# All modulation products on TensorE in float32, spread over four column bands

## The chip, the core and the metric

The kernel runs on one core of a Trainium2 chip. The core has five engines with a queue each: TensorE (PE in the profile; its weight loads are PEld), VectorE (DVE), ScalarE (ACT), GpSimd (POOL) and SyncE (SP), whose queue issues the transfers. The metric is the device time of one execution in microseconds; the figure of a kernel is the median of its runs.

## The reference, cut to what matters

Two layers work on 256 latent tokens and 256 context tokens of width 1024. In each layer a conditioning vector for the latents (`c`) and one for the context (`c_ctx`) give six modulation vectors of 1024 numbers: shift, scale and gate of the token mixing (parts 0, 1, 2) and of the channel mixing (parts 3, 4, 5).

```
silu_c, silu_cc = silu(c), silu(c_ctx)
for l in range(2):
    sh1, sc1, g1, sh2, sc2, g2 = split(silu_c @ w_mod[l] + b_mod[l], 6)      # latents
    csh1, csc1, cg1, ... = split(silu_cc @ w_mod[l] + b_mod[l], 6)           # context
    h = layer_norm(x) * (1 + sc1) + sh1
    x = layer_norm(ALPHA * x + g1 * token_mixer(h @ w_in[l]))
    h = layer_norm(x) * (1 + sc2) + sh2
    x = layer_norm(ALPHA * x + g2 * channel_mixer(h))
```

`w_mod[l]` is 1024 x 6144 in float32. The token mixer joins a Hyena, a Conformer and an S5 branch; the channel mixer is a dense SwiGLU in layer 0 and eight SwiGLU experts, two per token, in layer 1. In layer 1 only the latents are carried on behind the token mixer.

## The kernel before

All large products are three float32r products each: operands are split into a high part (a copy on ACT, line 123) and a low part (a subtraction on DVE, line 124), and lines 131 to 133 issue high-high, low-high and high-low. `p` tiles are the input projection, `bo` the branch outputs, `fo` and `pa` the two sides of the feed-forward.

A modulation part has two halves of 512 columns (`mods_half`, line 759). A half reads its weights in four chunks `mw` of 512 KB, each with two contraction steps of 128 rows, and goes one of two ways:

- the `fast` way: eight float32 products (line 781) with the two silu vectors as a stationary operand of two columns, into two rows of a PSUM tile `md`; ACT copies the two rows (line 793), four transposes (line 796) turn them into columns;
- the other way: DVE multiplies and accumulates each chunk by the scalar of its row (lines 785 and 787) into `ma`, for one or for both conditioning vectors; then a product with a column of ones (line 799), four to eight a half, sums over the 128 rows.

Both end in an addition of the bias on DVE (line 801) into `mo`.

Of layer 0, parts 0 and 1 (four halves) go the fast way at the very start, ahead of `prepare`, which needs them; part 2 goes fast, and parts 3 to 5 on DVE, in the background of the merge. All of layer 1's twelve halves go by DVE in the background of layer 0's feed-forward, side by side with `s5_pre(1)`, the preparation of layer 1's S5 branch. Background work is written as generators: `pump(n)` takes `n` steps of them (a chunk is a step) at fixed places of the foreground's loops: three for each pair of columns of the merge, three for each `f` of the feed-forward. A scheduler orders each engine's queue at build time from a simulated timeline; on the chip the queues keep that order. The PSUM tag `mm` has six banks, shared by `p`, `bo`, `fo`, `pa`, `md` and `mt`. The chunks' tiles are taken from the tags `XL` (six buffers, in the merge) and `Y` (four, in the feed-forward), and `ma` from the same tag.

Of the kernel before, what the change touches and what calls it, by code (L numbers as in the profile page):

```python
# [10 lines left out]
FT = mybir.dt.float32  # L11
# [3 lines left out]
OP = mybir.AluOpType  # L15
# [4 lines left out]
KD = 8  # L20
# [28 lines left out]
def tables():  # L49
    f32 = np.float32  # L50
    c = {}
    c["ident"] = np.eye(128, dtype=f32)
    t = np.arange(256)
    f = np.arange(256)
    w = 2 * np.pi * np.mod(np.outer(t, 2 * f + 1), 1024) / 1024.0
# [6 lines left out]
    for d in range(2):  # L62
        for k in range(8):
            ex[d * 64:(d + 1) * 64, k] = 7 - k if d == 0 else k
            ex[d * 64:(d + 1) * 64, 8 + k] = k + 1 if d == 0 else 8 - k
    c["exps"] = ex
    c["ramp"] = np.broadcast_to(np.arange(64, dtype=f32), (128, 64)).copy()
    tt = t.astype(f32)[:, None]
# [5 lines left out]
    for i in range(8):  # L74
        for tp in range(8):
            for ch in range(16):
                k = i - tp
# [13 lines left out]
class Net:  # L91
# [660 lines left out]

    def mods(self, l, part, tag="Y", fast=False):


        for h in range(2):
            yield from self.mods_half(l, part, h, fast, tag)

    def mods_half(self, l, part, h, fast, tag):

        nc = self.nc
        if h == 0:
            self.mo[l, part] = self.md.tile([128, 8, 2], FT, name=f"mo{part}", tag=f"mo{part}", bufs=2)
        mo = self.mo[l, part]
        bm = self.sm.tile([128, 4], FT, name="bm", tag="bm", bufs=4)
        nc.sync.dma_start(bm, self.i["b_mod"][l, part, :, 4 * h:4 * h + 4])
        if part % 3 == 1:
            nc.vector.tensor_scalar(bm, bm, 1.0, None, op0=OP.add)
        w0 = 0 if l == 0 or part < 2 else 1
        if fast:  # L770
            pp = self.ps("md")
        else:
            ac = self.t4([128, 2, 512], "ma", tag)
        for c in range(4):
            w = self.t4([128, 1024], "mw", "Z" if fast and tag == "XL" and h == 1 and c > 1 and part == 0 else tag)
            nc.sync.dma_start(w, self.i["w_mod"][l, 2 * part + h, c])
            for j in range(2):
                k = 2 * c + j
                wk = w[:, j * 512:(j + 1) * 512]
                if fast:  # L780
                    nc.tensor.matmul(pp[0:2], self.sv[:, k], wk, start=k == 0, stop=k == KD - 1)
                    continue
                for t in range(w0, 2):
                    if k == 0:
                        nc.vector.tensor_scalar(ac[:, t], wk, self.sv[:, k, t:t + 1], None, op0=OP.mult)
                    else:
                        nc.vector.scalar_tensor_tensor(ac[:, t], wk, self.sv[:, k, t:t + 1], ac[:, t],  # L787
                                                       op0=OP.mult, op1=OP.add)
            yield
        tp = self.ps("mt")  # L790
        if fast:
            row = self.t2([2, 512], "mrow")
            nc.scalar.copy(row, pp[0:2])
        for j in range(4):
            if fast:
                nc.tensor.transpose(tp[:, 2 * j:2 * j + 2], row[:, j * 128:(j + 1) * 128], self.ident[0:2, 0:2])
                continue
            for t in range(w0, 2):
                nc.tensor.matmul(tp[:, 2 * j + t:2 * j + t + 1], ac[:, t, j * 128:(j + 1) * 128], self.one,
                                 start=True, stop=True)  # L800
        nc.vector.tensor_tensor(mo[:, 4 * h:4 * h + 4, w0:],
                                tp[:, :8].rearrange("p (t w) -> p t w", w=2)[:, :, w0:],
                                bm[:, :, None].to_broadcast([128, 4, 2 - w0]), op=OP.add)

# [562 lines left out]
    def mixer(self, l, xin):  # L1367

        nc = self.nc
# [18 lines left out]
        if full:  # L1388
            self.bg = [self.mods(0, p, "XL", fast=p == 2) for p in range(2, 6)]
            self.rate = 3  # L1390
# [11 lines left out]
    def body(self, dbg=None):  # L1402
        nc, tc = self.nc, self.tc
# [15 lines left out]
        c = self.const  # L1419
# [7 lines left out]
        self.hl = self.big.tile([128, KD, 512], FR, name="hl", tag="hl", bufs=1)  # L1427
        self.sv = c.tile([128, KD, 2], FT, name="sv")
        with tc.high_priority():
# [5 lines left out]
        nc.vector.memset(self.ones512, 1.0 / 512.0)  # L1435
        self.one = c.tile([128, 1], FT, name="one")
        nc.vector.memset(self.one, 1.0)
        self.ident = c.tile([128, 128], FT, name="ident")
# [8 lines left out]
        with tc.high_priority():  # L1447
            m = [self.mods_half(0, p // 2, p % 2, True, t)
                 for p, t in enumerate(("XL", "XL", "Y", "XC"))]
            for _ in range(3):  # L1450
                next(m[0], None)
            xr = self.load_x(self.i["xin"], al, "Q")
            for g in m:
                self.run(g)
            self.prepare(xr, (0, 1), self.mo[0, 0], self.mo[0, 1])
# [43 lines left out]
def pack(inputs):  # L1499
    f32 = np.float32  # L1500
    I = {k: np.asarray(v) for k, v in inputs.items()}
# [4 lines left out]
    p["xin"] = C(tok.reshape(4, 128, 1024).transpose(1, 0, 2))  # L1506
    p["cv"] = C(np.stack([I["c_ctx"], I["c"][0]], -1).reshape(8, 128, 2).transpose(1, 0, 2))

# [64 lines left out]
```

## Time and profile before

| | us |
|---|---|
| median of three runs | 2623.72 |
| lowest, highest | 2621.29, 2623.99 |
| profiled execution, its own time | 2638.14 |
| span of the profiled execution | 2636.3 |
| PE busy in the span | 2435.7 (92%) |
| PEld busy | 2029.3 (77%) |
| DVE busy | 2162.4 (82%) |
| ACT busy | 1373.0 (52%) |

Busy times are sums of the records of an engine; matmuls are pipelined and their ends are modelled, so two records of PE overlap and a busy PE is not PE at its peak. What tells more is the step from one start to the next. A float32 product shows as two PEld and two PE records. "PEclk" is the TensorE clock that was granted, as a share of 2.4 GHz; a stretch at 1.2 GHz counts 0.5.

### The profile page before, as it was taken

The numbers are of one execution on the slowest core, as the hardware profiler recorded it, in microseconds if no ns is written. First come the engines' busy times: TensorE is split into PE (matmuls) and PEld (weight loads), VectorE is DVE, ScalarE is ACT, GpSimd is POOL, SyncE is SP. The second block draws the span as 40 slices with busy tenths as digits, with TensorE's granted clock in tenths as the row PEclk, the third lists the DMA queues.
The fourth block names the chain that finished last, engine by engine and source line by source line (L and its number), as shares of the span: only waits on it lengthen the run. The fifth ranks groups of instructions, "written<-read, shape, count | busy, mean of one in ns | idle before, by whom it ended". The sixth has DMA issues, their size and how long they took to land. (4 is left out here: it accounts for less than half of the span.)

```text
span 2636.3 us, 34684 instructions
## 1 busy us (share of the span) xinstructions
PE 2435.7 (92%) x12312; PEld 2029.3 (77%) x12312; DVE 2162.4 (82%) x3182; ACT 1373.0 (52%) x1951; POOL 191.5 (7%) x202
## 2 busy tenths in 40 slices
PE   7888999999899998996999969999999999999986
PEld 2765886788787777885898958888887788878775
DVE  7886789994758988756789778888988789888997
ACT  3343442323453232323444527777877677777864
POOL 1620010000100022211000010000000000000000
PEclk8998899999999999997889979999999999999998
DMA  7455425542325554553545529998999898999984
GB/s 261 156 193 132 160 81 176 176 159 90 108 93 169 184 176 156 197 200 134 188 139 155 179 73 374 354 350 341 351 344 347 329 338 340 351 351 357 359 321 201
DMA packets 147349, 602.52 MB, mean 229 GB/s; under 512 B 41878, under 2 KB 42584, under 8 KB 104160
## 3 DMA queue, kind: packets, MB, share of 16 engines
q1 hardware_dynamic: 147168, 600.24, 63.9%
q8 instruction: 98, 1.61, 0.2%
q14 instruction: 83, 0.68, 0.1%
HBM read 563.96 MB, written 36.21 MB: 228 GB/s over the span
## 5 line engine op out<-in xcount | busy, mean ns | idle before, releaser
L124 DVE TENSOR_TENSOR mwl<-mland,mwh 128x1024 fp32r<-128x1024 f32 x672 | 788.6, 1220 | 79.1 <-ACT mwh L123 65.6
L123 ACT CAST mwh<-mland 128x1024 fp32r<-128x1024 f32 x672 | 675.2, 1052 | 122.6 <-PE mp L133 37.0
L123 ACT CAST wh<-land 128x512 fp32r<-128x512 f32 x396 | 244.6, 621 | 527.7 <-PE p L132 241.4
L124 DVE TENSOR_TENSOR wl<-land,wh 128x512 fp32r<-128x512 f32 x396 | 285.3, 723 | 119.4 <-ACT wh L123 109.2
L131 PE MATMUL p<-hh,wh 128*128 128x256 f32 (+1 forms) x800 | 277.9, 348 | 14.2 <-DVE q L549 8.9
L133 PE MATMUL p<-hh,wl 128*128 128x256 f32 (+1 forms) x800 | 278.2, 350 | 7.0 <-DVE wl L124 6.5
L132 PE MATMUL p<-hl,wh 128*128 128x256 f32 (+1 forms) x800 | 275.5, 345 | 0.1
L1154 PE MATMUL mp<-mwl,xg 128*128 128x512 f32 x560 | 223.9, 402 | 5.2 <-DVE mwl L124 5.1
L1154 PE MATMUL mp<-mwh,xg 128*128 128x512 f32 x560 | 221.2, 397 | 3.5 <-ACT mwh L123 2.8
L787 DVE SCALAR_TENSOR_TENSOR ma<-mw,sv,ma 128x512 f32<-128x512 f32 x196 | 153.5, 806 | 37.1 <-DMA mw<-in_w_mod 36.8
L131 PEld LDWEIGHTS p<-hh,wh 128*128 128x128 f32 x800 | 157.1, 197 | 34.2 <-issue 9.2
L131 PE MATMUL mp<-mwh,xg 128*128 128x512 f32 x448 | 178.0, 397 | 2.6 <-ACT mwh L123 2.6
L132 PE MATMUL mp<-mwl,xg 128*128 128x512 f32 x448 | 177.7, 397 | 1.7 <-DVE mwl L124 1.6
L133 PEld LDWEIGHTS p<-hh,wl 128*128 128x128 f32 x800 | 156.7, 196 | 28.8 <-DVE wl L124 12.0
L133 PE MATMUL mp<-mwh,xg 128*128 128x512 f32 x448 | 176.4, 394 | 0.0
L132 PEld LDWEIGHTS p<-hl,wh 128*128 128x128 f32 x800 | 157.1, 196 | 15.9 <-DVE hl L751 0.3
L133 PE MATMUL fo<-hh,wl 128*128 128x512 f32 (+1 forms) x384 | 147.4, 385 | 1.7 <-DVE wl L124 1.7
L131 PE MATMUL fo<-hh,wh 128*128 128x512 f32 (+1 forms) x384 | 147.6, 385 | 1.3 <-ACT hh L747 0.5
L132 PE MATMUL fo<-hl,wh 128*128 128x512 f32 (+1 forms) x384 | 146.1, 381 | 0.1
L669 DVE SCALAR_TENSOR_TENSOR dc<-ub,cfp,dc 128x512 f32<-128x512 f32 (+1 forms) x240 | 142.9, 622 | 0.6
L1154 PEld LDWEIGHTS mp<-mwl,xg 128*128 128x128 f32 x560 | 106.5, 190 | 30.9 <-DVE mwl L124 10.3
L1154 PEld LDWEIGHTS mp<-mwh,xg 128*128 128x128 f32 x560 | 106.5, 190 | 24.7 <-ACT mwh L123 4.6
(460 smaller groups left out, 4926.9 us busy)
## 6 DMA issues: line engine op xcount, KB each, us to landing
mland<-in_moe_w SPq DMA_DIRECT2D x336, 1024.0 KB, 6.9
mw<-in_w_mod SPq DMA_DIRECT2D x96, 512.0 KB, 3.5
land<-in_w_in SPq DMA_DIRECT2D x96, 512.0 KB, 3.6
land<-in_ffn_w SPq DMA_DIRECT2D x66, 512.0 KB, 4.0
land<-in_w_bo SPq DMA_DIRECT2D x24, 512.0 KB, 3.5
s5we<-weT SPq DMA_DIRECT2D x16, 512.0 KB, 4.0
s5wc<-sw SPq DMA_DIRECT2D x16, 512.0 KB, 2.9
we<-s5we SPq DMA_DIRECT2D x16, 512.0 KB, 5.7
```

What stands on the lines that cost most here:

```text
L123: nc.scalar.copy(h, src)
L124: nc.vector.tensor_sub(lo, src, h.bitcast(FT))
L131: nc.tensor.matmul(o, a[0], b[0], start=start, stop=False)
L132: nc.tensor.matmul(o, a[0], b[1], start=False, stop=False)
L133: nc.tensor.matmul(o, a[1], b[0], start=False, stop=stop)
L669: nc.vector.scalar_tensor_tensor(d, ub[:, :R, i:i + 64], cfp[:, j, i:i + 1], d, op0=OP.mult, op1=OP.add)
L787: nc.vector.scalar_tensor_tensor(ac[:, t], wk, self.sv[:, k, t:t + 1], ac[:, t], op0=OP.mult, op1=OP.add)
L1154: self.nc.tensor.matmul(o, x[0][:, i], w[r], start=start and r == 0, stop=stop and r == 1)
```

## The change

All halves go to TensorE, in float32. The eight contraction steps `k` of a half are spread over four bands of 32 array columns, `k % 4` choosing the band: each product has 32 stationary columns (`sv` from column `2 * k` on, the two vectors of step `k` first, then those of the steps behind it or zeros) and writes the 32 rows of its band in the PSUM tile `md`. Each band sums two steps. ACT copies all 128 rows, and four float32 products with `pick`, a 0/1 matrix of 128 x 2 that takes rows 0 and 1 of each band, sum the bands and turn rows into columns in one. The DVE products, the product with ones and the `fast` flag are gone; both conditioning vectors are always made.

```diff
-    def mods_half(self, l, part, h, fast, tag):
+    def mods_half(self, l, part, h, tag, late=None):
...
-        w0 = 0 if l == 0 or part < 2 else 1
-        if fast:
-            pp = self.ps("md")
-        else:
-            ac = self.t4([128, 2, 512], "ma", tag)
+        pp = self.ps("md")
         for c in range(4):
-            w = self.t4([128, 1024], "mw", "Z" if fast and tag == "XL" and h == 1 and c > 1 and part == 0 else tag)
+            w = self.t4([128, 1024], "mw", late if late and c > 1 else tag)
             nc.sync.dma_start(w, self.i["w_mod"][l, 2 * part + h, c])
             for j in range(2):
                 k = 2 * c + j
-                wk = w[:, j * 512:(j + 1) * 512]
-                if fast:
-                    nc.tensor.matmul(pp[0:2], self.sv[:, k], wk, start=k == 0, stop=k == KD - 1)
-                    continue
-                for t in range(w0, 2):
-                    if k == 0:
-                        nc.vector.tensor_scalar(ac[:, t], wk, self.sv[:, k, t:t + 1], None, op0=OP.mult)
-                    else:
-                        nc.vector.scalar_tensor_tensor(ac[:, t], wk, self.sv[:, k, t:t + 1], ac[:, t],
-                                                       op0=OP.mult, op1=OP.add)
+                q = slice(32 * (k % 4), 32 * (k % 4) + 32)
+                nc.tensor.matmul(pp[q], self.sv[:, 2 * k:2 * k + 32], w[:, j * 512:(j + 1) * 512], start=k < 4, stop=k >= 4)
             yield
+        row = self.t2([128, 512], "mrow")
+        nc.scalar.copy(row, pp)
         tp = self.ps("mt")
-        if fast:
-            row = self.t2([2, 512], "mrow")
-            nc.scalar.copy(row, pp[0:2])
         for j in range(4):
-            if fast:
-                nc.tensor.transpose(tp[:, 2 * j:2 * j + 2], row[:, j * 128:(j + 1) * 128], self.ident[0:2, 0:2])
-                continue
-            for t in range(w0, 2):
-                nc.tensor.matmul(tp[:, 2 * j + t:2 * j + t + 1], ac[:, t, j * 128:(j + 1) * 128], self.one,
-                                 start=True, stop=True)
+            nc.tensor.matmul(tp[:, 2 * j:2 * j + 2], row[:, j * 128:(j + 1) * 128], self.pick, start=True, stop=True)
...
-            self.bg = [self.mods(0, p, "XL", fast=p == 2) for p in range(2, 6)]
+            self.bg = [self.mods(0, p, "XL") for p in range(2, 6)]
...
-        self.sv = c.tile([128, KD, 2], FT, name="sv")
+        self.sv = c.tile([128, 48], FT, name="sv")
...
-        self.one = c.tile([128, 1], FT, name="one")
-        nc.vector.memset(self.one, 1.0)
+        self.pick = c.tile([128, 2], FT, name="pick")
+        nc.sync.dma_start(self.pick, self.i["pick"])
```

## Rows read from the trace of the kernel before

**Rows 1.** Busy time by stage: window, length, each engine (count), clock, DMA share, GB/s.
```profile
0.00:44.00 44.00, 32.62 (x81) 6.57 (x81) 32.30 (x104) 14.14 (x18) 4.83 (x15) 0.96 0.92 339
44.00:250.00 206.00, 168.09 (x822) 133.15 (x821) 164.14 (x228) 82.61 (x146) 64.56 (x44) 0.89 0.49 154
...
430.00:780.00 350.00, 335.60 (x1577) 271.19 (x1575) 269.66 (x454) 127.37 (x212) 12.88 (x17) 0.95 0.39 130
780.00:1198.00 418.00, 395.58 (x1895) 330.15 (x1893) 327.05 (x542) 126.65 (x215) 67.25 (x46) 0.96 0.54 180
```

**Rows 2.** Timeline of PE in the merge: start, length, operation, count.
```profile
455.20 3.60 PE L781 MATMUL md<-mw,sv 128*2 128x512 f32 x8
458.73 0.50 PE L131 MATMUL p<-hh,wh 128*128 128x512 f32 x1
...
462.00 0.40 PE L133 MATMUL p<-hh,wl 128*128 128x512 f32 x1
462.23 0.39 PE L131 MATMUL p<-hh,wh 128*128 128x512 f32 x1
```

**Rows 3.** Groups of PE, 780 to 1198 us: count, busy us, mean ns, idle before.
```profile
L133 PE MATMUL fo<-hh,wl 128*128 128x512 f32 x292 | 117.1, 402 | 1.7 <-DVE wl L124 1.7
...
L133 PE MATMUL pa<-wh,fgL 128*128 128x512 f32 x176 | 70.1, 400 | 0.0
```

**Rows 4.** What PE waited for, 780 to 1198 us: total us, times, longest.
```profile
PE mp L330 <- DVE kf L311: 10.1, 2, 7.3
PE kp L305 <- DVE sw L290: 2.7, 1, 2.7
PE mt L799 <- DVE ma L787: 2.2, 1, 2.2
PE pa L132 <- DVE wl L124: 2.1, 2, 1.1
```

**Rows 5.** Three slices of 20 us, columns as in rows 1.
```profile
960.00:980.00 20.00, 17.16 (x79) 15.37 (x78) 13.89 (x18) 3.37 (x6) 12.81 (x10) 0.74 0.66 221
1000.00:1020.00 20.00, 12.74 (x62) 11.10 (x62) 19.88 (x23) 3.66 (x7) 14.22 (x10) 0.74 0.49 169
590.00:610.00 20.00, 18.81 (x73) 16.63 (x74) 6.68 (x12) 6.78 (x13) 0.18 (x1) 0.61 0.02 4
```

**Rows 6.** Groups of DVE: 780 to 1198 us, then 430 to 620 us.
```profile
L787 DVE SCALAR_TENSOR_TENSOR ma<-mw,sv,ma 128x512 f32<-128x512 f32 x112 | 94.2, 854 | 37.1 <-DMA mw<-in_w_mod 36.8
...
L785 DVE TENSOR_SCALAR ma<-mw,sv 128x512 f32<-128x512 f32 x16 | 8.6, 550 | 3.5 <-DMA mw<-in_w_mod 3.5
...
L787 DVE SCALAR_TENSOR_TENSOR ma<-mw,sv,ma 128x512 f32<-128x512 f32 x84 | 59.3, 741 | 0.0
...
L785 DVE TENSOR_SCALAR ma<-mw,sv 128x512 f32<-128x512 f32 x12 | 5.2, 474 | 0.0
```

**Rows 7.** Timeline of PE around the end of one half.
```profile
507.50 1.84 PE L799 MATMUL mt<-one,ma 128*128 128x1 f32 x16
509.20 0.48 PE L133 MATMUL p<-hh,wl 128*128 128x512 f32 x1
```

**Rows 8.** Groups of PE over the whole span.
```profile
L781 PE MATMUL md<-mw,sv 128*2 128x512 f32 x96 | 45.6, 626 | 8.5 <-DMA mw<-in_w_mod 8.5
...
L799 PE MATMUL mt<-one,ma 128*128 128x1 f32 x224 | 28.5, 251 | 2.2 <-DVE ma L787 2.2
...
L672 PE MATMUL mu<-dc,ones 128*128 128x512 f32 x8 | 4.1, 592 | 0.0
```

**Rows 9.** Timeline of PE at the start.
```profile
35.60 0.41 PE L796 MATMUL mt<-ident,mrow 2*128 2x2 f32 x4 [0.85 <-ACT mrow L793]
35.94 7.03 PE L781 MATMUL md<-mw,sv 128*2 128x512 f32 x16
```

**Rows 10.** Timeline of SP's queue at the start.
```profile
19.70 2.98 SPq L776 DMA_DIRECT2D mw<-in_w_mod  x4
```

**Rows 11.** Who waited for the chunks of line 776, 780 to 1200 us.
```profile
  DVE ma L787: 36.8, 18
```

More of the change, by code (lines that the diff above doesn't have):

```diff
@@ L66, in tables @@
     c["exps"] = ex
+    c["pick"] = np.tile(np.eye(32, 2, dtype=f32), (4, 1))
     c["ramp"] = np.broadcast_to(np.arange(64, dtype=f32), (128, 64)).copy()
@@ L751, in modulate, with mods @@
                 nc.vector.tensor_sub(self.hl[:, k, cs], f[:, j], self.hh[:, k, cs].bitcast(FT))
-    def mods(self, l, part, tag="Y", fast=False):
+    def mods(self, l, part, tag="Y"):
         for h in range(2):
-            yield from self.mods_half(l, part, h, fast, tag)
-    def mods_half(self, l, part, h, fast, tag):
+            yield from self.mods_half(l, part, h, tag)
+    def mods_half(self, l, part, h, tag, late=None):
         nc = self.nc
@@ L778, in mods_half @@
                 k = 2 * c + j
-                wk = w[:, j * 512:(j + 1) * 512]
-                if fast:
-                    nc.tensor.matmul(pp[0:2], self.sv[:, k], wk, start=k == 0, stop=k == KD - 1)
-                    continue
-                for t in range(w0, 2):
-                    if k == 0:
-                        nc.vector.tensor_scalar(ac[:, t], wk, self.sv[:, k, t:t + 1], None, op0=OP.mult)
-                    else:
-                        nc.vector.scalar_tensor_tensor(ac[:, t], wk, self.sv[:, k, t:t + 1], ac[:, t],
-                                                       op0=OP.mult, op1=OP.add)
+                q = slice(32 * (k % 4), 32 * (k % 4) + 32)
+                nc.tensor.matmul(pp[q], self.sv[:, 2 * k:2 * k + 32], w[:, j * 512:(j + 1) * 512], start=k < 4, stop=k >= 4)
             yield
+        row = self.t2([128, 512], "mrow")
+        nc.scalar.copy(row, pp)
         tp = self.ps("mt")
-        if fast:
-            row = self.t2([2, 512], "mrow")
-            nc.scalar.copy(row, pp[0:2])
         for j in range(4):
-            if fast:
-                nc.tensor.transpose(tp[:, 2 * j:2 * j + 2], row[:, j * 128:(j + 1) * 128], self.ident[0:2, 0:2])
-                continue
-            for t in range(w0, 2):
-                nc.tensor.matmul(tp[:, 2 * j + t:2 * j + t + 1], ac[:, t, j * 128:(j + 1) * 128], self.one,
-                                 start=True, stop=True)
-        nc.vector.tensor_tensor(mo[:, 4 * h:4 * h + 4, w0:],
-                                tp[:, :8].rearrange("p (t w) -> p t w", w=2)[:, :, w0:],
-                                bm[:, :, None].to_broadcast([128, 4, 2 - w0]), op=OP.add)
+            nc.tensor.matmul(tp[:, 2 * j:2 * j + 2], row[:, j * 128:(j + 1) * 128], self.pick, start=True, stop=True)
+        nc.vector.tensor_tensor(mo[:, 4 * h:4 * h + 4], tp[:, :8].rearrange("p (t w) -> p t w", w=2),
+                                bm[:, :, None].to_broadcast([128, 4, 2]), op=OP.add)
     def row(self, cols, r, tag="aux", bufs=2):
@@ L1447, in body @@
         with tc.high_priority():
-            m = [self.mods_half(0, p // 2, p % 2, True, t)
+            m = [self.mods_half(0, p // 2, p % 2, t, "Z" if p == 1 else None)
                  for p, t in enumerate(("XL", "XL", "Y", "XC"))]
@@ L1506, in pack @@
     p["xin"] = C(tok.reshape(4, 128, 1024).transpose(1, 0, 2))
-    p["cv"] = C(np.stack([I["c_ctx"], I["c"][0]], -1).reshape(8, 128, 2).transpose(1, 0, 2))
+    cv = np.stack([I["c_ctx"], I["c"][0]], -1).reshape(8, 128, 2).transpose(1, 0, 2).reshape(128, 16)
+    p["cv"] = np.pad(cv, ((0, 0), (0, 32)))
     def cols(w):
```

## The prediction

> **What bounds the kernel now.** I read the busy time by stage first [rows 1]. The change touches three places: the start (0 to 44 us), where the modulation vectors of layer 0's parts 0 and 1 are made; layer 0's merge and projection (430 to 780 us); and layer 0's feed-forward (780 to 1198 us), under which layer 1's twelve halves are made. After that no modulation product is left. In the second and third stage TensorE is 96% and 95% busy, DVE 77% and 78%. A busy TensorE proves little, since its records overlap, so I looked at the steps between starts. Two float32r products of 512 columns start 0.227 us apart (462.00 to 462.23) [rows 2]. In the feed-forward the `fo` products (292 on one line, three such lines) and the `pa` products (176, three lines) [rows 3] are 1404 of them: 1404 x 0.227 = 319 us. The other 491 of its 1895 instructions there [rows 1] are mostly short ones; at 0.106 us (the price of a short one, below) they are 52 us, so TensorE has work for at least 371 of 418 us. The rest is switching, waiting and slow clock: its waits for DVE sum to 17.1 us in the four rows of [rows 4], and in two slices of 20 us the granted clock was 0.74 [rows 5], that is 10.4 us at the 1.2 GHz level in each, of which half, 5.2 us, is lost. So TensorE is the bound here, and DVE delays it only in places. Layer 0's merge looks the same, with one hole: at 590 to 610 us the clock was 0.61, 15.6 us at the lower level, 7.8 us lost.
>
> **What goes from DVE.** The 112 + 16 accumulations of the feed-forward took 94.2 + 8.6 us and the 84 + 12 of the merge 59.3 + 5.2 [rows 6]: 167 us of DVE. None of it is time by itself; it is worth what TensorE waited for. In the feed-forward that is at most 17.1 us of waits plus 10.4 us of lost clock beside them, 27.5 us. I take 24, since most of the waits are for `kf` and `sw`, behind which these accumulations stand in DVE's queue. In the merge the convolution's taps share DVE with the accumulations; when it ends earlier, its statistics no longer stand alone at 590 us, and I take the 7.8 us as 8. DVE's relief: -32 (bounds 0 and -35).
>
> **What goes to TensorE: the vectors' ends.** Before, a half ends in 8 or 16 instructions of a 128x128 load and one column; 16 of them took from 507.50 to 509.20 us, 0.106 us each [rows 7]. There are 224 [rows 8]: -23.7 us. The 24 transposes cost 0.085 us each (four from 35.60 to 35.94) [rows 9]; 8 of them fall into the merge: -0.7. The new band sum is four float32 products a half, two instructions each, of the same load and two columns, so by the same row 0.106: 160 in the two late stages, +17.0. Sum -7.4; at the start 32 of these for 16 transposes, +2.0. The copy of 128 rows for 2 rows costs ACT the same 512 columns, and ACT is busy 36% and 30% of the two stages [rows 1]: nothing, because it has the room; the half's result is needed much later.
>
> **What goes to TensorE: the products.** A float32 product of 512 columns is two instructions, each 0.43 to 0.44 us: 16 took 7.03 us [rows 9], 8 took from 455.20 to 458.73 [rows 2]. The mean of `mu`, which loads 128 columns, is 592 ns, and that of `md`, which loads 2, is 626 with its slow-clock starts [rows 8]: so a narrow load makes a product no cheaper, and 32 columns cost what 2 do. The late stages get 20 halves of 8 calls, 320 instructions; today 32 of them (part 2) are there, 13.8 us. One after another the new ones are 137.6 us: +123.8. No row shows two products in different bands of 32 columns, so their overlap is unknown. The lower bound is four bands independent of each other.
>
> How the calls lie decides what overlap can give. A chunk of 512 KB brings two calls, for two neighbouring bands; each call is a first and a second pass into its own band, and the second must wait for the first. If instructions start in the order of the queue, the first pass of the second call can run beside the second pass of the first call, and nothing else can: three slots of 0.43 us where one after another it is four. If two chunks stand together, it is five slots for eight. I take the middle, 2.75 slots or 1.18 us a chunk: 80 chunks are 94.6 us, +80.8. Independent bands would make two slots of a lone chunk (68.8 us, +55.0) and two of a pair of chunks (34.4 us, +20.6).
>
> The Trainium skill, page "TensorE: Matmul & The Clock Gate", Part 3, reports three column bands of 32 columns and 512 moving columns at 2.38 times one band's rate. No row here shows it; by that figure the products would be an estimated 57.8 us, and the sum +7 where I say +44. The same section says that matmuls start and end in the order of the program, which is the condition of my three slots; the rows here agree that nothing on one band overtakes.
>
> **Switches.** Four or eight narrow products between wide ones cost about 0.09 us beyond their 0.43 each (455.20 to 458.73 is 3.53 us for 8) [rows 2]. 72 chunks are new in the late stages: +6.5. Lower bound 0, when chunks stand together.
>
> **The start.** The four halves run one after another on TensorE, the last products from 35.94 for 7.03 us [rows 9], while the last four weight chunks were issued from 19.70 on [rows 10] and the DMA share was 0.92. With overlap the products keep up with the chunks, and the modulation can begin up to 12 us earlier. But from 44 to 250 us DVE is busy 80% and the clock 0.89 [rows 1], so part of it is given back to DVE's own chain: I take -6 (0 to -12). Without overlap it is 0. The two small loads (`pick`, a wider `sv`) hide under the wait for the first chunk.
>
> **The sum.** Products +80.8, ends -7.4 and +2.0, switches +6.5, DVE's relief -32, start -6: +44 us. The profiled execution was 2638.14 us (span 2636.3), 14 above the median of 2623.72; the sum is of one execution's differences and I add it to the median: 2668 us.
>
> **Rivals.** *One after another*: bands don't overlap for float32. Then the products cost +123.8 and the start gains nothing: 123.8 - 7.4 + 2.0 + 6.5 - 32 = +93, 2717 us. For it: no row shows any two products sharing the array. Against it: nothing either. *Four bands at once*: products +20.6 to +55.0, the rest as in the sum: -16 to +18, and with all of the 27.5 us and all of the start about -26, so 2597 to 2642 us. This is the one that ends on the other side. It decides at a price: the sum is zero when a chunk costs 0.63 us ((13.8 + 7.4 - 2.0 - 6.5 + 32 + 6) / 80), so it is faster only if neighbouring chunks share the array too; a lone chunk of two calls can't fall below 0.86. *The late chunk*: DVE waited 36.8 us in 18 times for weight chunks [rows 11]. These waits pass to TensorE, which keeps its order and has the feed-forward's products behind them. The buffer that the accumulator held is freed for a fourth chunk, which speaks against it; in full it would add 36.8 to the sum, +81, 2705 us. The half's accumulator also holds one of six PSUM banks through four chunks, while `pa` needs four and `fo` two; I can't price that and count it here. *The change does nothing*: would need a price per chunk by accident at 0.63; counted under the bands.
>
> **Chances.** In-order overlap 0.37 (2668, own range 2640 to 2690), one after another 0.25, four bands at once 0.31, late chunk 0.07. The range: 2600 to 2722, from the better part of four bands to the slot-by-slot case. 0.2% is 5 us, about what a measurement of this kernel can tell from no change. Faster: 0.20 of the four bands' 0.31, and 0.07 of the in-order case, where DVE's relief and the start would have to be worth twice what I took: 0.27. Within 5 us: 0.10. Slower: 0.63.
>
> **What the profile will show.** Right, if the starts of two `md` instructions of different bands coincide but never more than two, and 16 of them take 3.9 to 5.2 us; if DVE falls by some 165 us and the stages of rows 1 nevertheless grow, the feed-forward by 25 to 40 us. Wrong, if 16 of them still take 6.9 us or as little as 1.8, if TensorE waits for `mw` in the feed-forward, or if the `kf` waits and the 0.74 slices stay although DVE is free. The prediction fails most easily on the overlap, which no row of before prices, and next on the 32 us of relief.

## The result, and the profile after

The changed kernel took 2645.38 us (median of 6 runs, 2636.04 to 2650.53), the kernel before 2622.81 (6 runs) beside it: ratio 1.0082, 95% interval 1.0063 to 1.0101. That is 22 us slower, where 44 slower was predicted. The same kernel later came out at 1.0049 (e10) and 1.0039 (e18), 13 and 10 us slower; over the three, 1.0057 or 15 us is what there is to explain. The profiled execution took 2649.37 us, 2647.6 of it the span.

Busy time by stage in the profile after, columns as in [rows 1]; the first four lines answer to [rows 1], the last three to [rows 5]:

```profile
0.00:44.00 44.00, 25.37 (x115) 12.35 (x116) 30.96 (x101) 15.63 (x23) 4.48 (x15) 0.71 0.91 333
44.00:250.00 206.00, 170.30 (x794) 131.71 (x793) 164.18 (x226) 80.62 (x142) 73.03 (x44) 0.85 0.45 151
430.00:780.00 350.00, 334.70 (x1606) 261.87 (x1605) 205.29 (x348) 131.59 (x220) 12.46 (x17) 0.96 0.39 124
780.00:1198.00 418.00, 408.11 (x2007) 318.79 (x2005) 246.66 (x407) 128.59 (x221) 65.94 (x46) 0.98 0.53 178
590.00:610.00 20.00, 20.00 (x84) 13.34 (x84) 8.39 (x15) 5.82 (x11) 0.00 (x0) 0.86 0.35 110
960.00:980.00 20.00, 20.00 (x116) 15.85 (x115) 19.25 (x28) 5.91 (x11) 7.34 (x8) 1.00 0.57 184
1000.00:1020.00 20.00, 20.00 (x101) 15.83 (x100) 8.95 (x14) 3.72 (x6) 0.00 (x0) 1.00 0.44 156
```

VectorE lost 64 us in the merge and 80 in the feed-forward. The two bad slices of the feed-forward are healed: TensorE is busy through both, at a granted clock of 1.00 where it was 0.74. The merge's bad slice is not healed but spread: from 590 to 610 us the clock is 0.86 where it was 0.61, but in the 20 us ahead of it 0.80 where it was 0.96. By the clock, 13.6 of these 40 us are at the lower level, before 17.2.

```profile
570.00:590.00 20.00, 17.46 (x90) 15.13 (x89) 5.32 (x9) 9.77 (x16) 1.02 (x1) 0.80 0.31 101
```

The waits of TensorE from 780 to 1198 us, against [rows 4]: `kf` and `sw` are gone, and nothing large has taken their place:

```profile
PE kh L132 <- ACT hh L124: 3.4, 2, 2.1
PE mt L783 <- ACT mrow L780: 2.0, 2, 1.2
PE h L515 <- DVE h L517: 1.5, 2, 1.3
PE md L777 <- DMA mw<-in_w_mod: 1.1, 1, 1.1
```

The new products, in TensorE's timeline (start, length, operation, count of instructions; a call is two instructions). They answer to [rows 2, 7, 9]:

```profile
31.25 1.99 PE L777 MATMUL md<-mw,sv 128*32 128x512 f32 x16
...
441.32 0.95 PE L783 MATMUL mt<-pick,mrow 128*128 128x2 f32 x8
442.20 1.06 PE L777 MATMUL md<-mw,sv 128*32 128x512 f32 x8
443.20 0.50 PE L132 MATMUL p<-hh,wh 128*128 128x512 f32 x1
...
798.88 1.05 PE L777 MATMUL md<-mw,sv 128*32 128x512 f32 x4 [1.10 <-DMA mw<-in_w_mod]
799.87 0.50 PE L132 MATMUL pa<-wh,fgH 128*128 128x512 f32 x1
```

Read the steps between starts. Eight instructions, that is two chunks or four calls in four bands, hold TensorE from 442.20 to 443.20: 1.00 us, where eight took 3.53 before [rows 2]. Four instructions, a lone chunk, hold it from 798.88 to 799.87: 0.99 us. The other groups of this trace agree: where nothing is waited for, groups of two, four, six and eight instructions take 0.98, 0.98, 0.99 and 1.00 us. Two calls cost as much as four: the bands run side by side, and a lone chunk leaves two of them empty. A whole half is 1.99 us where it was 7.03 [rows 9].

So products and picks are cheap. Over 410 to 1240 us, all new products (line 777) and then all picks (line 783) are, by busy time, count, then loads, clock, DMA share and GB/s:

```profile
410.00:1240.00 830.00, 55.74 (x320) 8.53 (x320) 0.95 0.46 152
410.00:1240.00 830.00, 20.43 (x160) 20.79 (x160) 0.95 0.46 152
```

In the kernel before the same window held 32 product instructions (line 781), 224 ends (line 799) and 8 transposes (line 796):

```profile
410.00:1240.00 830.00, 14.38 (x32) 2.38 (x32) 0.94 0.46 155
410.00:1240.00 830.00, 28.52 (x224) 30.77 (x224) 0.94 0.46 155
410.00:1240.00 830.00, 0.81 (x8) 0.64 (x8) 0.94 0.46 155
```

Products cost 41.4 us more and ends 8.9 less. That alone does not tell where the time went, because the stages after 1231 us, which the change doesn't touch, are longer as well. Two groups of TensorE mark them (minimum, median and longest ns, then first and last start in us): the last transpose of the layer-0 output into the second mixing (`tp`), and the experts' first product (`mp`). In the profile after:

```profile
L741 PE MATMUL tp<-ident,xr x64: 270/421/476, 38.9 to 1231.1; 128*128 128x128 f32 x64
L132 PE MATMUL mp<-mwh,xg x448: 388/389/782, 1593.8 to 2519.9; 128*128 128x512 f32 x150
```

and in the profile before:

```profile
L740 PE MATMUL tp<-ident,xr x64: 270/418/476, 44.0 to 1231.2; 128*128 128x128 f32 x64
L131 PE MATMUL mp<-mwh,xg x448: 387/389/735, 1589.0 to 2505.6; 128*128 128x512 f32 x150
```

In these two executions everything that the change touches ends at the same time, 1231.1 and 1231.2. From there to `mp` is 362.7 us after and 357.8 before; from `mp` to the end of the span 2647.6 - 1593.8 = 1053.8 after and 2636.3 - 1589.0 = 1047.3 before. The whole difference of the two spans, 11.3 us, lies where no modulation product is left. The program that builds the kernel orders the instructions of each engine anew for each version: in the traces, 0.93 of TensorE's entries (runs of like instructions) behind the last `tp` stand in the same sequence as in the kernel before. From this came the two theories that the runs were made for. *Late order*: much of the loss is the other order of the second mixing and the experts. *In place*: the loss is TensorE's new work, and what it leaves behind.

### The profile page after: what moved, and what is told of

Read it like the earlier page. It is cut to its first block, busy times and chain, and to the rows that moved or that the text cites. A ratio compares the mean times of both kernels' runs of the same rounds, so it can differ in the third digit from the quotient of the medians.

```text
span 2647.6 us, 34950 instructions
## 1 busy us (share of the span) xinstructions
PE 2458.5 (93%) x12544; PEld 2026.7 (77%) x12544; DVE 2029.5 (77%) x2957; ACT 1384.4 (52%) x1969; POOL 198.0 (7%) x202
## 5 line engine op out<-in xcount | busy, mean ns | idle before, releaser
L125 DVE TENSOR_TENSOR wl<-land,wh 128x512 fp32r<-128x512 f32 x396 | 295.9, 750 | 244.3 <-ACT wh L124 243.0
L1136 PE MATMUL y<-mwh,gh 128*128 128x512 f32 x280 | 114.6, 417 | 6.3 <-DVE gh L125 6.3
```

Of the source, the lines that this page charges most:

```text
L125: nc.vector.tensor_sub(lo, src, h.bitcast(FT))
L1136: self.nc.tensor.matmul(o, x[0][:, i], w[r], start=start and r == 0, stop=stop and r == 1)
```

## The experiments

All runs in one table. The three stretches are of the profiled execution, from the two groups above and the span; the ratio is to the kernel before, run beside it on the same chip.

| run | what | ratio (95%) | to last `tp` | to first `mp` | to the end |
|---|---|---|---|---|---|
| before | | 1 | 1231.2 | 357.8 | 1047.3 |
| e3 | before, again | one run | 1220.9 | 357.3 | 1045.4 |
| e9 | before, fills ahead of the router | 1.0016 (1.0003 to 1.0029) | 1223.2 | 358.4 | 1047.9 |
| after | | 1.0082 (1.0063 to 1.0101) | 1231.1 | 362.7 | 1053.8 |
| e4 | after, again | one run | 1221.7 | 359.0 | 1053.6 |
| e10 | after, third time | 1.0049 (1.0031 to 1.0067) | 1231.1 | 359.6 | 1051.7 |
| e18 | after, fourth time | 1.0039 (1.0021 to 1.0057) | 1230.6 | 363.9 | 1053.9 |
| e7 | after, TensorE's late order as before | 1.0011 (0.9993 to 1.0030) | 1218.9 | 360.6 | 1050.0 |
| e16 | e7 again | 1.0009 (0.9994 to 1.0024) | 1229.5 | 361.1 | 1045.7 |
| e17 | e7 with more fills | 1.0014 (0.9999 to 1.0030) | 1218.7 | 357.8 | 1045.5 |
| e11 | after, pick a step later | 1.0066 (1.0049 to 1.0083) | 1232.2 | 359.5 | 1047.0 |
| e15 | after, chunks in pairs | 1.0032 (1.0014 to 1.0050) | 1226.1 | 356.4 | 1047.7 |
| e8 | after, 8 halves back on VectorE | 1.0036 (1.0018 to 1.0054) | 1232.7 | 358.3 | 1042.6 |
| e1 | before, with stop | 1.0036 (1.0022 to 1.0051) | 1215.4 | 368.3 | 1046.6 |
| e12 | before, with stop, again | 1.0026 (1.0010 to 1.0042) | 1216.8 | 364.7 | 1047.0 |
| e2 | after, with stop | 1.0067 (1.0050 to 1.0084) | 1218.0 | 368.3 | 1049.5 |
| e13 | after, with stop, again | 1.0058 (1.0036 to 1.0079) | 1225.9 | 370.9 | 1050.3 |
| e14 | after, with stop, chunks in pairs | 1.0058 (1.0037 to 1.0080) | 1215.8 | 367.7 | 1046.3 |
| e5 | after, with stop, one band | 1.0319 (1.0285 to 1.0352) | 1299.7 | 363.1 | 1053.0 |
| e6 | after, with stop, sums on VectorE too | 1.0112 (1.0080 to 1.0143) | 1239.3 | 369.7 | 1047.1 |

One program's first stretch moves by 10 us from execution to execution (1231.2 and 1220.9; 1231.1 and 1221.7), its last two by some 2 to 5. So the first stretch is settled by timing, and the late ones can be read from profiles.

Part of what moves lies ahead of the first `bo`, the first product of the branch outputs: in the kernel before it starts at 417.3 and at 408.1 (e3). From there to the last product of the feed-forward, `pa`, three profiles without the change and without a stop (before, e3, e9) have 773.8 to 774.8 us, the changed kernel's four 774.2 to 783.7. Behind that last `pa` TensorE waits for the layer norm `xr`, in the kernel before and in the changed one alike. The first transpose starts 21.0 us behind it in the kernel before and 20.7 in the changed one, whose last two halves run inside this wait. The kernel before, then the changed one:

```profile
1192.18 2.74 PE L799 MATMUL mt<-one,ma 128*128 128x1 f32 x24
1213.16 2.25 PE L740 MATMUL tp<-ident,xr 128*128 128x128 f32 x8 [18.24 <-ACT xr L714]
```

```profile
1194.37 1.92 PE L777 MATMUL md<-mw,sv 128*32 128x512 f32 x16
...
1201.64 5.39 PE L777 MATMUL md<-mw,sv 128*32 128x512 f32 x16 [3.51 <-DMA mw<-in_w_mod]
...
1212.83 2.25 PE L741 MATMUL tp<-ident,xr 128*128 128x128 f32 x8 [4.06 <-ACT xr L715]
```

So what the change puts there, two halves of products and three picks in place of 24 ends, costs nothing: by busy time 7.7 us of the 32.5 that products and ends add.

**Equal order behind the change (e1, e2, e12, e13).** A stop of all engines stands ahead of the second mixing. It costs some time itself, and behind it the engines of both kernels have the same instructions in the same order (so the traces of e1, e2, e12 and e13). In e5 and e6 below, which have the stop too, TensorE's order behind it agrees with e2's in only 0.82 and 0.93 of its entries, so their prices are read ahead of the stop.

```diff
+            tc.strict_bb_all_engine_barrier()
             xr, gb = self.mixer(1, xs)
```

e1: 

> The kernel before with one line more: all engines meet once, ahead of layer 1's token mixing, so that the instruction order behind that point no longer depends on what stood ahead of it. It is the base for the next run. Both theories: some us slower than the kernel before through the meeting itself (0 to +15 us), unless the late order that it gets is worth something of its own.

e2: 

> The changed kernel with the same line; behind it, its instruction order on every engine is that of the run with the line in the kernel before. Theory 'late order' (the changed stages end where they ended, and the 22 us come from another instruction order in layer 1's mixing and the experts): within 6 us of the kernel before with the line. Rival 'in place' (the products and ends on TensorE cost it in the merge and the feed-forward): 15 to 25 us slower than the kernel before with the line.

e12: 

> The kernel of e1 again, as the partner of the next two on one chip: 2630 to 2640. Behind the stop the three issue the same instructions in the same order on every engine.

e13: 

> The kernel of e2 again. Products by its rows 0.71 us a chunk, 0.53 when two chunks stand together and 1.0 when one stands alone. Theory (in place the change costs something): 3 to 14 over the partner, as the first pair's 8 plus or minus 6. Rival (in place it costs nothing): within 3 of it.

Medians of e1 and e2 were 2635.39 and 2643.48, of e12 and e13 2631.90 and 2642.61. By the ratios the change costs 0.0031 and then 0.0032, 8.1 and 8.4 us, with some 6 and 7 us of uncertainty each: with an equal order behind it, the change is slower by about 8 us (4 to 13). That is about half of the free order's 15, and not nothing: neither theory alone. The profiles say the same: from the first `bo` to the last `pa` 775.8 and 779.4 us with the change, 772.2 and 768.4 without, 7 us more.

**The two kernels again (e3, e4, e10, e18).** No edit.

e3: 

> The kernel before, unchanged, for a second profile: its profiled execution was 14 us above its median. 'Late order': the 14 us lie behind 1198 us (experts' transfers), the stages up to 1198 us repeat within 2 us, and the span is near 2621. 'In place': some of the 14 us lie ahead of 1198 us, so that the profile of before hid a loss there.

e4: 

> The changed kernel, unchanged, for a second profile. 'Late order': the feed-forward's last product again ends near 1192 us, as in the kernel before, and the difference to the second profile of before, some 15 to 25 us, lies in layer 1's mixing and the experts. 'In place': it is there at 1198 us.

e10: 

> The changed kernel once more, unaltered, on the chip and in the hour of the other kernels of this call. Both theories: a ratio near 1.008; mixing near 293 us and experts near 1024.

e18: 

> The changed kernel unaltered, partner of e16 and e17: ratio 1.005 to 1.008, stretches of 360 and 1053 us behind the last tp.

e3 took 2625.42 us and e4 2636.09; the medians of e10 and e18 were 2638.94 and 2640.63, a little less of a loss than expected. Ahead of the last `tp` both kernels' profiles differ by 10 us from one execution to the next, so the two first profiles do not tell what the change does there. The last stretch repeats: 1047.3 and 1045.4 before; 1053.8, 1053.6, 1051.7 and 1053.9 after, 6.9 us more on average. The middle one adds 3.8 (357.6 and 361.3). Together the late stretches are 10.7 us longer.

**The change without its late order, and the order without the change (e7, e16, e17, e9).** Repeated fills of a constant (0.165 us each on VectorE, from 572 us on in e7's trace) shift what the builder does behind them. Thirty of them on the changed kernel (e7, e16) or 45 (e17) leave TensorE's sequence ahead of the last `tp` as it was in 0.99 of its entries; behind it 0.98 stand as in the kernel before, where without the fills it is 0.93.

```diff
# e7, e16 (thirty times) and e17 (45 times), on the changed kernel
+            nc.vector.memset(self.ones512, 1.0 / 512.0)
             xr, gb = self.mixer(1, xs)
# e9 (thirty times), on the kernel before
+            nc.vector.memset(self.ones512, 1.0 / 512.0)
             rest = self.route(xr)
```

e7: 

> The changed kernel, without a stop, with 30 repeated fills of a 128x128 constant on VectorE ahead of the second layer's mixing (same value, nothing else changed). They shift the order that the build gives the late stages: TensorE's is then the order of the kernel before in all but a few rows. Theory late order (some 14 of the 22 us come from the order behind the changed stages): second mixing and experts come back from 293 and 1024 us to 288 and 1015, and the time is 2630 to 2638, the fills' own 0 to 6 us in it. Rival (the 22 us belong to the products and to what they leave behind, such as a cooler clock): 2645 as the changed kernel, or up to 6 more.

e16: 

> The kernel of e7 again: the change with thirty fills, TensorE's order ahead of the second mixing that of the changed kernel in 0.99, behind it that of the kernel before in 0.98. Late order: 10 to 18 us below e18 on this chip, ratio 1.000 to 1.003. Rival (e7's 1.0011 was a good hour, and the order is worth only the 3 us that e7's late stretches are shorter in its profile): 1.004 to 1.006.

e17: 

> The same with 45 fills, whose order is that of e16 but for the place of the fills. Late order: as e16, within 4 us. Rival: as e18 less 3.

e9: 

> The kernel before, with 30 repeated fills of a 128x128 constant on VectorE just ahead of the router (same value, nothing else changed). All that lies ahead of the router keeps its order; in the experts TensorE's order moves from that of the kernel before to one that is close to the changed kernel's. Theory late order: the experts (first to last start of their first matmul) take 1020 to 1025 us in place of 1015, with the mixing's 288 unchanged, and the time is 5 to 12 over the kernel before, of which the fills can make at most 6. Rival (the order of these stages is worth nothing, the loss in them comes from what the products leave behind): experts 1015, time within 4 of the kernel before.

The late order carries half of the loss or more. The medians of e7, e16 and e17 are 2631.51, 2629.91 and 2630.97, the ratios 1.0011, 1.0009 and 1.0014: 3 us over the kernel before, at the edge of what can be told, though every product is still on TensorE and 5 or 7 us of fills are on VectorE. e16 and e17 ran beside e18 and stand 8 and 7 us under it by the ratios, where at least 10 were expected; e18 itself was one of the changed kernel's better results. Over all six the difference is 12 of the 15 us. In the profiles the two late stretches together are 1406.9 us on average in these three, 1414.6 in the changed kernel's four and 1403.9 in the two of the kernel before: 8 us of the 12 are found behind the last `tp`. The other 4 are not found there; ahead of it these three have 770.9 to 774.5 us from the first `bo` to the last `pa`, the changed kernel 774.2 to 783.7, with TensorE's order almost the same, so that part may be chance. e7's profile alone was no proof, since its last stretch (1050.0) was only half the way back; the last stretches of e16 and e17 are all the way back, and e17's middle one too:

```profile
L741 PE MATMUL tp<-ident,xr x64: 271/421/477, 38.6 to 1218.7; 128*128 128x128 f32 x64
L132 PE MATMUL mp<-mwh,xg x448: 387/389/774, 1576.5 to 2493.3; 128*128 128x512 f32 x150
```

That is e17, with a span of 2622.0: 357.8 and 1045.5, the numbers of the kernel before. e9 is the weak one: 4 us slower, about what its fills may cost, and the last stretch rose by 0.6 to 2.5 us where 5 or more were expected. Its order agreed with the changed kernel's in 0.96 of TensorE's last 3000 entries, but the kernel before itself agrees in 0.95: it had hardly moved, and it could not show what the changed kernel's order costs without the change. What makes that one order slow is not known.

**The pick a step later (e11).** Between the row copy and the pick one more step of the background work was put.

```diff
         nc.scalar.copy(row, pp)
+        if l or part > 1:
+            yield
         tp = self.ps("mt")
```

> The changed kernel with one more step between the row copy and the pick of the late halves, so that the pick's four products stand behind other work and don't wait for ScalarE's copy (8.6 to 9.7 us of such waits in the changed kernel's profiles). The order that the build gives from the second mixing on is, on TensorE, row for row that of e9. Theory: in place it saves 2 to 6 us against the changed kernel, and in the late stages it takes as long as e9 (within 3 us), so it stands 5 to 12 below the changed kernel if e9's order is better than that of the changed kernel, and at the changed kernel's time less 2 to 6 if it is as slow. Rival to late order: mixing and experts as in the changed kernel whatever the order, 2640 to 2645.

The edit did nothing for what it was for: TensorE waited for `mrow` 2.0 us in the feed-forward, as in the changed kernel. But it got another late order, on TensorE nearly that of e9 (0.99 of the entries behind the last `tp`, all of the last 3000) and of the kernel before (0.98). Its late stretches are 359.5 and 1047.0, e9's 358.4 and 1047.9. One of the two kernels has the products on VectorE, the other on TensorE; with nearly one order they take the same time in these stages, which is against anything that the products would leave behind. (The stop's pairs are not as clean: 3 us more in the last stretch in e2 and e13 than in e1 and e12, but not in e14.) What it lost, at 2640.47, its profile puts into the first stretch (1232.2): two more halves now run behind the feed-forward's last `pa`, four in place of two, and the first transpose comes 31.7 us behind it where it was 20.7. So the order ahead of the second mixing counts too.

**One band (e5).** All eight steps of a half go to one column group.

```diff
-                q = slice(32 * (k % 4), 32 * (k % 4) + 32)
-                nc.tensor.matmul(pp[q], ..., start=k < 4, stop=k >= 4)
+                nc.tensor.matmul(pp[0:32], ..., start=k == 0, stop=k == KD - 1)
```

> The changed kernel with the stop of e2, but all eight product steps of a half go into one column group (start at the first, stop at the last); the row copy and the pick then read 32 partitions in place of 128. Theory (four column groups run at once, about 1.0 us for four calls): undone, eight calls of 0.86 us follow one another, 6.9 us a half where the profile of the changed kernel has 1.9 to 2.0; 20 late halves give +95, the four at the start some more, so 2735 to 2755, and 16 products in a row show 13.8. Rival one, the prediction's step (a waiting second pass stops the queue, 1.18 us a chunk, 4.7 a half): then the spread saves only 2.2 us a half and this kernel loses 45 at most, 2675 to 2695. Rival two (the products are hidden behind other waits): within 5 us of e2.

Median 2716.8, ratio 1.0319. By the ratios that is 66 us over e2, by the last `tp` 81.7, and from the first `bo` to the last `pa` 80.8 (856.6 for 775.8). TensorE's timeline shows a chunk (4 instructions) at 1.90 us where four bands took 0.99, and ten at 4.48:

```profile
458.31 2.76 PE L776 MATMUL md<-mw,sv 128*32 128x512 f32 x6
...
471.96 1.90 PE L776 MATMUL md<-mw,sv 128*32 128x512 f32 x4
...
491.54 4.48 PE L776 MATMUL md<-mw,sv 128*32 128x512 f32 x10
```

Its 20 late halves are 146.3 us of TensorE, in e2 53.6:

```profile
408.00:1310.00 902.00, 146.31 (x320) 31.83 (x320) 0.97 0.40 135
406.00:1310.00 904.00, 53.60 (x320) 8.33 (x320) 0.95 0.47 156
```

That is 92.7 us more. Two of the halves run in the wait behind the last `pa`, where their 7.2 us cost nothing (from the last `pa` to the last `tp` e5 takes 35.0 us, e2 35.4). The other 85.5 us moved the last `pa` by 80.8: 0.95 us of end for each us of work (0.92 by the same reckoning against e13). TensorE is the bound of these stages, as [rows 1 to 3] were read, and the spread over four bands works. By the whole time the price is lower, 66 us; part of the gap is that e5's late stretches are 2 us shorter than e2's and 5 shorter than e13's, in another order, and the rest is not explained. The time stayed below the 2735 expected because the expectation took 4.9 us for each of 20 halves, where 18 count and each is 4.6.

**VectorE's sums kept (e6).** VectorE makes the sums of the kernel before again, into an accumulator that takes its buffer again, and nothing reads them.

```diff
+                for t in range(w0, 2) if dve else ():
+                    ...
+                    nc.vector.scalar_tensor_tensor(ac[:, t], wk, self.sv[:, 2 * k + t:2 * k + t + 1], ac[:, t], op0=OP.mult, op1=OP.add)
```

> The changed kernel with the stop of e2, and VectorE makes the sums of the kernel before as well, for the same parts, though nothing reads them: its 167 us come back, TensorE's work stays. The prediction took the relief of VectorE as 32 us. If that is right, the waits for kf and sw and the slices at three quarters of the clock come back in the feed-forward, and the time is 2660 to 2680, nearly all of it ahead of the stop. Rival (VectorE's time was hidden and its relief worth next to nothing): within 5 us of e2's 2643.

Median 2659.9, ratio 1.0112: 13 us over the mean of e2 and e13, with some 9 of uncertainty; the last `tp` came 13 to 21 us later. In the feed-forward VectorE's busy time went back from 246.66 to 319.55 us:

```profile
780.00:1198.00 418.00, 406.21 (x1970) 317.03 (x1968) 319.55 (x505) 122.46 (x211) 68.11 (x44) 0.98 0.46 159
```

and TensorE's waits there are the splits of the weights, which stand behind the sums in VectorE's queue:

```profile
PE fo L134 <- DVE wl L125: 4.3, 5, 1.4
PE kh L132 <- ACT hh L124: 3.4, 2, 2.1
PE pa L133 <- DVE wl L125: 2.7, 1, 2.7
```

So the relief is real, but not 32 us: 13 by the ratios, 13 to 21 by the last `tp`. From the first `bo` to the last `pa` it is 11 to 14 (790.0 for 775.8 and 779.4). The other 7 of the profile lie behind the last `pa`, where the last halves' products wait 8.8 us for their chunks, longer than the wait for the layer norm hides; e2, with the products alone, and the kernel before, with the sums alone, show nothing like it. The waits for `kf` did not come back, nor did the clock (0.98 over the feed-forward): that part of the expectation missed.

**Eight halves back on VectorE (e8).** Parts 2 to 5 of the second layer, of which one column alone is needed, are summed on VectorE.

```diff
+        fast = l == 0 or part < 2
...
+                if not fast:
+                    for t in range(w0, 2):
+                        ...
+                    continue
```

> The changed kernel with parts 2 to 5 of the second layer (8 halves, of which one column alone is needed) back on VectorE as in the kernel before, all other halves on TensorE in four column groups. TensorE has 8 times (1.9 + 0.5 - 0.4) = 16 us less than in the changed kernel, VectorE 64 times 0.8 = 51 us more, in the feed-forward, where it was busy 247 us of 418. If VectorE's relief there is worth little, the changed stages end 10 to 16 us earlier than the changed kernel's; if it is worth what the products cost, they end at the same time. The late order is another again, so the total may move 10 us either way: 2625 to 2645; the stages ahead of the second mixing are what is compared.

Median 2637.83, ratio 1.0036, and its front is among the latest of all (1232.7), though TensorE has some 16 us less to do. TensorE's two longest waits from 780 to 1240 us and VectorE's group of the sums (count, busy us, mean ns, idle before):

```profile
PE tp L741 <- ACT xr L715: 20.6, 2, 18.2
PE fo L134 <- DVE wl L125: 10.8, 4, 5.5
```

```profile
L787 DVE SCALAR_TENSOR_TENSOR ma<-mw,sv,ma 128x512 f32<-128x512 f32 x56 | 52.2, 932 | 44.5 <-DMA mw<-in_w_mod 43.9
```

The first line is the wait behind the feed-forward again, as long as in the kernel before and now without work in it. The second is new: VectorE stood idle for 43.9 us ahead of the sums, waiting for chunks of the modulation weights, and the splits `wl` that TensorE needs stand in the same queue. TensorE waited 10.8 us for them, where the changed kernel had 1.0. That is two thirds of the 16 us. The total is lower than the changed kernel's by its late stretches (358.3 and 1042.6, together the shortest of all runs).

**Chunks in pairs (e14, e15).** The first chunk's calls are written behind the second chunk's load.

```diff
-            for j in range(2):
-                k = 2 * c + j
+            ws.append(w)
+            for k in (range(2 * c, 2 * c + 2) if l == 0 and part < 2 else range(2 * c - 2, 2 * c + 2) if c % 2 else ()):
...
+                wk = ws[k // 2][:, (k % 2) * 512:(k % 2 + 1) * 512]
```

e14: 

> The changed kernel with the same stop, and the products of a late half issued two chunks at a time (the first chunk's two calls wait until the second chunk has landed; loads are issued as before). Theory (four bands run at once, and a lone chunk wastes half of them): 20 halves at 2.1 us in place of 2.8, 13 us less of TensorE, and since 88 us more of it in e5 moved the end of the changed stages by 80, some 12 us less than e13. Rival (TensorE then waits for the second chunk, or the chunks' buffers come free later): e13's time or more, with waits for mw in the feed-forward above 5 us.

e15: 

> The same without the stop. The order of TensorE from the second mixing on is row for row that of e9 and e11, whose late stages took 1106 us from the last tp to the end, against 1103 to 1105 in the kernel before and 1111 to 1117 in the changed one. Theory: the changed stages 12 us below the changed kernel's and the late ones as e9's, so 2618 to 2628, at or a little below the kernel before. Rival as in e14: 2635 to 2645.

e14's median was 2642.55, as e13's; e15's 2635.80. Nothing was gained, because there was little to pair. In the changed kernel's timeline from 430 to 1240 us, 23 of the product groups are already of 8 instructions and 7 of 4; in e14 26 and 2. The products' busy time from 430 us on is 49.3 us in e14 and 53.4 in e13, 4 us less where 13 were expected. The builder had put most chunks side by side by itself. e15 takes e11's late order (all of TensorE's last 3000 entries) and again has its late stretches (356.4 and 1047.7); what it loses, 8 us by the ratio, is not in them. No version that was tried beat the kernel before.

## Why the prediction was right in sign and wrong in size

It gave the direction, and two to three times the size: +44 us, where +22 was measured at once and +15 over three measurements. And most of these 15 are not the loss that it predicted: in the changed stages it is 3 us (e7, e16, e17) to 8 (the stop's pairs, e15). That the sign came out is in good part luck: its products were priced 39 us too dear, its relief 11 to 21 too high, and the largest part of the measured loss has no term in it. Of its signs, the feed-forward grew by 3 to 7 us, from its first product to its last `pa` (468.9 and 469.2 before; 472.3 to 475.9), not by 25 to 40, and 16 instructions took 1.99 us, not 3.9 to 5.2.

**What bounds the kernel.** Right. In e5 a us of TensorE's work ahead of the last `pa` cost 0.95 us. What the sum had no room for is the wait of 20 us behind the last `pa`, in which two halves run for nothing.

**The products.** This is the step that failed: "If instructions start in the order of the queue, the first pass of the second call can run beside the second pass of the first call, and nothing else can". Passes of four calls run beside each other; 320 instructions took 55.74 us, 0.70 a chunk and not 1.18, and +41.4 in place of +80.8. This was the rival *four bands at once*, said to run from -16 to +18; it got 0.31 against 0.37. Its price of two slots for a lone chunk and two for a pair, 0.86 us, was nearly met: 0.99 and 1.00. Its turning point was 0.63 a chunk; at 0.70 the prediction's own sum is 44 - 80 x (1.18 - 0.70) = +5.6. In the text, the Trainium skill's page "TensorE: Matmul & The Clock Gate", Part 3, was cited for three bands at 2.38 times one band's rate, and the sum it gave was +7. Here eight instructions in four bands ran at 3.53 / 1.00 = 3.5 times one band's rate. The page's ordered starts, taken as the reason for three slots, do not keep calls of other bands waiting for a second pass.

**The ends.** -7.4 predicted, -8.9 measured. Right. The switches (+6.5) were nearly nothing: the first product behind a group is followed 0.33 us later where it is 0.23 otherwise, and the group's busy 1.06 already holds 0.06 of these 0.10.

**VectorE's relief.** The waits for `kf` and `sw` and the slow slices of the feed-forward went as said, but -32 was too much: making the sums again costs 11 to 14 us ahead of the last `pa`, 13 by timing (e6). The reason given fails too, since with the sums back neither the `kf` wait nor the slices at 0.74 came back. The 8 us for the merge had the least ground: its slow stretch stayed.

**The start.** The first `p` starts 5 to 6 us earlier (46.4 for 51.4, 44.9 for 50.8), and by the first `bo` most of that is gone: the ten profiles of kernels with the change and no stop have it at 406.1 to 417.3, the three without the change at 408.1 to 417.3. The text took -6, with half of the gain given back; nearly all of it was.

**One after another** (2717) is what e5 made: 2716.8. That they agree to the us is luck, as e5 has the stop and the rival's sum the relief of 32. **The late chunk** didn't come: TensorE waited 1.1 us for `mw` in the feed-forward, and another 3.5 inside the wait behind it. In e8 VectorE waits for late chunks, and in e6 TensorE does.

**What had no term.** The stages behind the change. The prediction said that after the feed-forward no modulation product is left, and stopped there. They gave 10.7 us of the loss by profiles; giving them the kernel before's order takes back 8 us by profiles and 12 by timing. That it goes with the order is shown by e7, e16 and e17, where most of it vanished with the products in place, and by e11 and e15, which with the change and nearly the kernel before's order have late times like those of e9 without it. By what wait the changed kernel's order is slow was not found.

**The sum, done again.** Products and ends add 41.4 - 8.9 = 32.5 us, of which 7.7 lie in the wait behind the last `pa`. The other 24.8 at 0.92 to 0.95 are 23 to 24; less 11 to 14 of relief, with nothing for the start, this gives +9 to +13 up to the last `pa`. The stop's pairs measured +7 there, single pairs from +4 to +11. So it closes within the scatter of the profiles. In the free order it does not: the changed kernel's four profiles are 4 us longer than those without the change, and e7, e16 and e17 2 us shorter. Part of that may be relief that e6 can't show, such as the sums' results, for which TensorE waited before [rows 4] and which in e6 nothing reads. That was not tried and stays open.

## What to carry to other kernels

A product with 32 or fewer output rows can be spread over four column groups, even in float32, and four calls then cost what one or two do (1.00 and 0.98 us here): price it by chunks that stand together, since a lone pair of calls costs as much as four. Look for a wait that the engine has anyway: work that lands in it is free, here two halves of 24. Work taken from an engine off the path is worth what the path waited for it, and to measure that, put the work back as dead work. Where the build orders instructions by itself, a change also reorders stages that it doesn't touch, here for 8 to 12 us, as much as the edit itself or more: divide the profile at a point behind the change, and compare versions with equal order (a stop, or an edit without work) before a small difference is put down to the edit.

## What was not expected of the hardware

VectorE lost 167 us of accumulations, but its busy time fell by 133 only (2162.4 to 2029.5 over the span). Other operations took longer: 396 splits `wl` 283.0 us in e3 and 296.2 in e4, and 32 products `bb` 16.1 and 28.5, with equal counts and shapes. The longer ones are those beside which GpSimd ran: splits that no GpSimd instruction overlaps take 683 ns on average in e3 and 689 in e4, those that one overlaps 1127 (31 of them) and 1259 (43). In the first 44 us the granted clock was 0.71 where it was 0.96 [rows 1] (0.80 in e4, 0.67 in e10, 0.96 in e3). With four bands TensorE was busy 25 us of these 44, before 33, and from 37 to 47 us, behind 3.9 us without work, the clock was 0.50, its level of 1.2 GHz; in the kernel before it was 1.00 from 30 to 47. Eight picks take 1.87 us there (from 37.17) and 0.95 at full clock (from 441.32).
